# A hybrid SSD and MLP block on one core: the scheduler's order made with its other simulation

## The chip, the cores and the metric

The kernel runs on one core of a Trainium2 chip. The metric is the device time of one execution in microseconds, the median of several runs; a single profiled execution gives the trace and the profile.

## The reference

One decoder block over 512 tokens of width 1024: adaLN modulation from a vector c, RMSNorm, then a mixer of two branches (a Mamba-2 scan in 4 groups and 4 chunks of 128 tokens, and a causal pooling over four windows), gates, an output projection, a second norm, a squared-ReLU MLP of width 4096 and a last norm.

```python
mod = (silu(c) @ w_ada + b_ada); shift_m, scale_m, gate_m, shift_f, scale_f, gate_f = split(mod, 6)
h = rmsnorm(x, norm_mix_w) * (1 + scale_m) + shift_m
z, xbc, dt_raw, u_pool, gate_logits = split(h @ w_in)
xs, b, c = split(silu(causal_conv4(xbc)))
dt = softplus(dt_raw + dt_bias)
y = ssd_chunked_scan(xs * dt, -exp(a_log) * dt, b, c) + d_skip * xs      # 4 groups, 4 chunks
y_ssd = group_rmsnorm(y * silu(z)) @ w_branch_ssd
y_pool = causal_multiscale_pool(u_pool) @ w_branch_pool
x = x + gate_m * ((sigmoid(g_ssd) * y_ssd + sigmoid(g_pool) * y_pool) @ w_out)
h = rmsnorm(x, norm_mlp_w) * (1 + scale_f) + shift_f
x = x + gate_f * (relu(h @ w_up) ** 2 @ w_down)
return rmsnorm(x, norm_final_w)
```

## The kernel before

**Matrix products.** Channels lie on the partitions, tokens in the free dimension, so a product's output tile is 128 x 512 in one PSUM bank. Every product is three passes: both factors are split into a high part (a copy to fp32r) and a low part (the difference), and `mm3` (L155, L156, L157) adds high x high, high x low and low x high. A `unit` is one 128-column block of a weight: `load_unit` loads 1024 numbers per partition on SP (L140), makes the high part on ACT (L145, a cast) and the low part on DVE (L146), and PE then runs 24 matmuls, 8 slices by 3 passes. Activations are split in the same way by `split` (L125 on ACT, L126 on DVE).

**Stages.** A head (up to L332, about 60 us) makes h and the first seven products of w_in; its order is written by hand (`manual_schedule`). L353 to L377 turn the dt columns into dt (softplus by a series on DVE), into its running sums (PE L369 and transposes L373), and ACT (L374, L375) and SP (L376, L377) write these to two DRAM tables, `cs_d` and `ecs_d`. Then come the units of w_in with conv (ACT L395, DVE L397, ACT L412 for silu) and gate silu (L439), and between them the four groups of the scan. `ssd_group` loads for every chunk a broadcast of `cs_d` (SP L490), masks it (POOL L495), exponentiates it on ACT (L492, L494, and eight L499), multiplies by the scores on DVE (L500), transposes xs (PE L503), makes the chunk's state by one mm3, copies it (ACT L537 for the first chunk, into s_143 in group 0), and adds the output from the state of the chunk before (PE L529) and the one within the chunk (PE L549). L586 to L590 are the group's norm; `bs` (L457) multiplies by w_branch_ssd. Pooling, gates and w_out follow. The second norm is made in two halves of the tokens: PE L777 sums squares, ACT L779 and L780 make the factor, and for each of the eight slices of h DVE L806, ACT L807 and DVE L808 make the scaled, the high and the low part, h2[k]. The MLP starts with `up_first` and four plain units; the rest of w_up is multiplied by Strassen-like `Pair`s of seven products (`product`, L893; 12 matmuls of 256 columns), whose results go through ACT L1001 (relu), L1002 (square), a cast L834 and DVE L835 into `us`; `down_plain` (matmuls L155 to L157, then DVE L1082) multiplies `us` by w_down, once for each quarter of the hidden width. `last_down` ends with DVE L1100, the squares (ACT L1061, L1064, L1067, DVE L1065), the norm (PE L777, ACT L779, L780), four DVE multiplications L1107 for each half and the output DMAs L1108.

**What sets the order.** The program is written as calls in one order, each tile in a slot of the kernel's own lists (`Slots`, first in, first out). The tile framework then fixes an order for each engine and each queue: it simulates the program and takes, at each step, an instruction that is ready, by program order and by priority (`high_priority`, `issue_after`). On the chip each engine then runs its list strictly in turn and waits at an instruction until its inputs are there. The context has two simulations for this; the flag is read at L1190, and nothing else of the kernel is seen in the order. Slots and waits follow from the program, so that both orders use the same tiles.

```python
def prepare(c):                                          # in ssd_group
    sp.dma_start(m, cs_d[heads, cc].partition_broadcast(P))          # L490
    ...
    for i in range(HG):
        act.activation(m[:, i, :], m[:, i, :], AF.Exp, ...)          # L499
    dve.tensor_tensor(m, m, sc[:, cc]..., ALU.mult)                  # L500
...
for k in range(8):                                       # second norm, for each half
    dve.scalar_tensor_tensor(t, x1[k][:, t0:t1], amod..., R[:, t0:t1], ...)   # L806
    act.activation(hi, t, AF.Identity, bias=shift)                            # L807
    dve.scalar_tensor_tensor(lo, t, shift, hi.bitcast(F32), ...)              # L808
```

## Time and profile before

| what | value |
|---|---|
| runs | 966.47, 966.64, 968.96 us; median 966.64 |
| profiled execution | 965.36 us, span 963.6 us |
| granted clock of TensorE | 0.998 of full speed |
| instructions | 13261 |
| HBM read, written | 126.13 MB, 2.23 MB |

The page gives busy time by engine, the span in 40 slices, the chain of work that ended last, and groups of instructions by line; the trace behind it also answers with a timeline (start, duration from the first start to the last end of a row's instructions, engine, line, operation, output and inputs, count, and in brackets the idle time ahead of it with what ended it), with busy time by stretches, and with waits. PE is the TensorE matmul queue, PEld its weight loads, DVE VectorE, ACT ScalarE, POOL GpSimd, SP the queue that issues DMAs. Matmuls are pipelined: a row's duration is longer than the distance to the next start.

### The profile page before, as it was taken

Reading aid. Unit: us, or ns where it says so; the run is one execution under the profiler, and the core shown is the slowest. Engines: PE = TensorE matmul, PEld = TensorE weight load, DVE = VectorE, ACT = ScalarE, POOL = GpSimd, SP = SyncE. Lnnn points to the kernel's source line nnn. Section 1 sums busy time; section 2 is a strip of 40 time slices with the busy share of each in tenths; the row PEclk is TensorE's granted clock in tenths of the full one; section 3 lists DMA queues with packets and bytes.
Section 4 is the critical chain, followed back from the end, with each engine's and each line's share of the span. In section 5 each row is a group of like instructions: output and inputs, shape, how many; then the busy total and the mean of one; then the engine's idle time right before and its main releaser. Section 6 shows DMA issues by size and latency. Waiting matters only on the chain.

```text
span 963.6 us, 13261 instructions
## 1 busy us (share of the span) xinstructions
PE 950.4 (99%) x5135; PEld 804.5 (83%) x5135; DVE 657.7 (68%) x961; ACT 499.6 (52%) x811; POOL 89.6 (9%) x91
## 2 busy tenths in 40 slices
PE   8999999999999999999999999999999999999996
PEld 5877878888888888788888888998899889889986
DVE  7978868467766787987567574795557556664633
ACT  6479975657528542563312452684247127425732
POOL 0102321220212132300000000000000000000000
PEclk9999999999999999999999999999999999999999
DMA  9746433433253334446578463242144225214002
GB/s 369 298 132 182 130 99 121 131 110 110 76 161 113 98 101 132 158 153 210 181 241 281 127 208 120 94 143 75 45 145 130 66 76 165 89 33 154 23 1 88
DMA packets 61761, 129.22 MB, mean 134 GB/s; under 512 B 4673, under 2 KB 29505, under 8 KB 61698
## 3 DMA queue, kind: packets, MB, share of 16 engines
q1 hardware_dynamic: 61696, 128.38, 41.7%
q8 instruction: 40, 0.66, 0.3%
q14 instruction: 23, 0.19, 0.1%
q10 hardware_dynamic: 2, 0.00, 0.0%
HBM read 126.13 MB, written 2.23 MB: 133 GB/s over the span
## 4 chain that ended last, share of the span: by engine, by line
PE 84%; DVE 8%; ACT 3%; DMA 2%; issue 2%; POOL 0%; SPq 0%; DVEq 0%; ACTq 0%; POOLq 0%
PE ps L155 21%; PE ps L156 21%; PE ps L157 21%; PE ps L893 12%; PE ps L328 4%; DVE d L146 1%; PE ps L549 1%; DMA d<-cs_d 1%; DVE s L126 1%; PE ps L529 1%; DVE d L171 1%; DVE pad L631 1%; PE ps L503 1%; DMA d<-xp 1%; ACT d L145 1%
## 5 line engine op out<-in xcount | busy, mean ns | idle before, releaser
L155 PE MATMUL ps<-s,d 128*128 128x512 f32 (+1 forms) x1080 | 412.1, 382 | 1.1 <-ACT s L649 0.6
L156 PE MATMUL ps<-s,d 128*128 128x512 f32 (+1 forms) x1080 | 408.1, 378 | 0.2 <-DVE s L126 0.2
L157 PE MATMUL ps<-s,d 128*128 128x512 f32 (+1 forms) x1080 | 407.9, 378 | 0.0
L155 PEld LDWEIGHTS ps<-s,d 128*128 128x128 f32 x1080 | 202.7, 188 | 42.1 <-issue 2.2
L157 PEld LDWEIGHTS ps<-s,d 128*128 128x128 f32 x1080 | 202.7, 188 | 38.2 <-issue 0.2
L156 PEld LDWEIGHTS ps<-s,d 128*128 128x128 f32 x1080 | 202.8, 188 | 37.5 <-DVE s L126 0.7
L146 DVE TENSOR_TENSOR d<-d,d 128x1024 fp32r<-128x1024 f32 x88 | 112.4, 1278 | 61.6 <-ACT d L145 56.8
L145 ACT CAST d<-d 128x1024 fp32r<-128x1024 f32 x88 | 92.0, 1046 | 115.3 <-PE ps L156 74.7
L893 PE MATMUL ps<-s,d 128*128 128x256 f32 x864 | 103.8, 279 | 0.0
L893 PEld LDWEIGHTS ps<-s,d 128*128 128x128 f32 x864 | 102.9, 188 | 0.2
L834 ACT CAST d<-d 128x1024 fp32r<-128x1024 f32 x44 | 45.8, 1050 | 88.5 <-PE ps L156 62.8
L835 DVE TENSOR_TENSOR d<-d,d 128x1024 fp32r<-128x1024 f32 x44 | 53.5, 1223 | 27.4 <-ACT d L834 18.8
L834 ACT CAST d<-sz 128x1024 fp32r<-128x1024 f32 x32 | 33.7, 1052 | 68.9 <-PE ps L156 48.9
L1082 DVE SCALAR_TENSOR_TENSOR xs<-ps,mod,xs 128x512 f32<-128x512 f32 x29 | 21.8, 750 | 69.6 <-PE ps L157 69.6
L171 DVE CUSTOM_DVE_ANT_0 d<-d,d,par_t 128x1024 f32<-128x1024 f32 x32 | 41.8, 1307 | 27.3 <-DMA d<-adaT 27.2
L835 DVE TENSOR_TENSOR d<-sz,d 128x1024 fp32r<-128x1024 f32 x32 | 39.2, 1224 | 19.7 <-ACT d L834 16.4
L328 PE MATMUL ps<-s,d 128*128 128x512 f32 x168 | 40.1, 391 | 1.9 <-ACT s L316 1.9
L499 ACT ACTIVATE d<-d,ncs 128x128 f32<-128x128 f32 x128 | 39.9, 391 | 4.0 <-POOL d L495 4.0
L397 DVE SCALAR_TENSOR_TENSOR s<-ps,par_t,s 128x511 f32<-128x511 f32 (+2 forms) x54 | 39.7, 742 | 0.3
L328 PEld LDWEIGHTS ps<-s,d 128*128 128x128 f32 x168 | 31.4, 188 | 9.6 <-ACT s L316 2.4
L125 ACT CAST s<-s 128x512 fp32r<-128x512 f32 x32 | 19.7, 619 | 31.2 <-POOL s L511 18.7
L126 DVE TENSOR_TENSOR s<-s,s 128x512 fp32r<-128x512 f32 x32 | 25.7, 807 | 4.5 <-ACT s L125 4.5
(219 smaller groups left out, 1005.7 us busy)
## 6 DMA issues: line engine op xcount, KB each, us to landing
d<-adaT SPq DMA_DIRECT2D x32, 512.0 KB, 4.2
d<-wx SPq DMA_DIRECT2D x18, 512.0 KB, 3.6
d<-wdn SPq DMA_DIRECT2D x18, 512.0 KB, 3.9
d<-cs_d SPq DMA_DIRECT2D x16, 512.0 KB, 6.1
d<-wbs SPq DMA_DIRECT2D x16, 512.0 KB, 3.5
d<-wgate SPq DMA_DIRECT2D x16, 512.0 KB, 4.2
d<-wz SPq DMA_DIRECT2D x15, 512.0 KB, 3.5
sz<-wdn SPq DMA_DIRECT2D x14, 512.0 KB, 4.3
```

The source lines that it names most:

```text
L145: act.copy(hi[:, :w], r[:, a:a + w])
L146: (low or dve).tensor_tensor(lo[:, :w], r[:, a:a + w], hi[:, :w].bitcast(F32), ALU.subtract)
L155: pe.matmul(ps, whi, xhi[:, t0:t1], start=start, stop=False)
L156: pe.matmul(ps, whi, xlo[:, t0:t1], start=False, stop=False)
L157: pe.matmul(ps, wlo, xhi[:, t0:t1], start=False, stop=stop)
L171: dve.tensor_tensor_reduce(r, r, cbc, 1.0, col("b_ada", j), ALU.mult, ALU.add, mod[:, j:j + 1])
L328: pe.matmul(first[u], w[u][i // 2], h[k][i % 2], start=k == 0 and i == 0, stop=k == 7 and i == 2)
L397: dve.scalar_tensor_tensor(t[:, sh:], ps[:, :T - sh], w(3 - sh), t[:, sh:], ALU.mult, ALU.add)
L499: act.activation(m[:, i, :], m[:, i, :], AF.Exp, bias=ncs[:, c, g * HG + i:g * HG + i + 1])
L834: act.copy(dst[0], src)
L835: dve.tensor_tensor(dst[1], src, dst[0].bitcast(F32), ALU.subtract)
L893: pe.matmul(ps, x, y, start=start and m == 0 and i == 0, stop=m == 3 and i == 2, skip_group_check=True)
```

## The change

One argument at L1190: the context makes the order with its other simulation, the one that follows the queues in time. No instruction is added or removed by the program (the framework places 38 activation-table loads on ACT where it placed 36); what changes is the order on each engine and on SP's queue.

```diff
-    with tile.TileContext(nc) as tc:
+    with tile.TileContext(nc, schedule_with_timeline_sim=True) as tc:
         block_kernel(tc, out=out, **args)
```

The head keeps its order up to the first unit, and so do the last matmuls. In between some things move in every stage. In group 0 of the scan the whole chain L356 to L377 goes behind conv work, and PE's L369 from ahead of the unit of ps_118 to the end of that of ps_149; the DMAs L376, L377 and L490 go behind five weight loads; the L549 and L529 of the chunks go one or two units later, into the units of ps_192, ps_201 and ps_206; group 0's norm sum (L586) goes behind the first products of group 1. In groups 1 to 3 the L529 and L549 move up among the units of w_branch_ssd, and many sets are cut in pieces. In the second norm DVE takes eight L806 and then eight L808 where it took them by threes. In the Pair stages the products are taken in another order.

On ACT, in group 0, before: from the exponentials of the second chunk (d_130) to the copy L537 of the first chunk's state, and what stood behind it.

```order
L499 ACTIVATE d_130_742<-d_130_742,ncs 128x128
L145 CAST d_190_1103<-d_189_1101 128x1024
L499 ACTIVATE d_130_742<-d_130_742,ncs 128x128 x7
L125 CAST s_134_768<-s_133_766 128x512
L537 COPY s_143_813<-ps_142_809 128x512
L395 ACTIVATE s_150_864<-ps_149_839,par_t 128x512
L412 ACT_TABLE_LOAD
```

And now: the last twelve rows up to the same copy. Ahead of them stand, as before, the first chunk's exponentials (d_124) and the split L125 of s_128.

```order
L494 ACT_TABLE_LOAD
L494 ACTIVATE dec_80<-dec_80 128x8
L499 ACTIVATE d_130_742<-d_130_742,ncs 128x128 x8
L125 CAST s_134_768<-s_133_766 128x512
L499 ACTIVATE d_152_872<-d_152_872,ncs 128x128 x8
L145 CAST d_212_1247<-d_211_1245 128x1024
L125 CAST s_156_898<-s_155_896 128x512
L439 ACT_TABLE_LOAD
L439 ACTIVATE sz_178_1031<-ps_182_1038 128x512
L412 ACTIVATE xs_158_902<-s_163_934 128x512
L412 ACTIVATE xs_158_902<-s_174_1005 128x512
L537 COPY s_143_813<-ps_142_809 128x512
```

The copy L537, which stood right behind the second chunk's split (s_134), now has the third chunk's exponentials, two table loads, a weight cast and the silus L439 and L412 of later units ahead of it.

On PE, at the end of the first Pair stage, before: the last matmul of the last Pair's last product (ps_1082), and then the unit pair of down_plain (ps_1095 and ps_1096) from its first slices, us[0] (s_950, s_951), on.

```order
L893 MATMUL ps_1082_6377<-s_1007_5745,pad_1081_6323 128x256
L156 MATMUL ps_1095_6516<-s_951_5512,d_1086_6428 128x512
L157 MATMUL ps_1095_6516<-s_950_5511,d_1087_6429 128x512
L155 MATMUL ps_1096_6517<-s_950_5511,d_1089_6434 128x512
L156 MATMUL ps_1096_6517<-s_951_5512,d_1089_6434 128x512
L157 MATMUL ps_1096_6517<-s_950_5511,d_1090_6435 128x512
L155 MATMUL ps_1095_6516<-s_952_5513,d_1086_6428 128x512
```

And now: behind the same matmul stand the last two slices of that unit pair, us[6] (s_962, s_963) and us[7] (s_964, s_965); the rest of the unit pair has gone between the Pair's products.

```order
L893 MATMUL ps_1082_6377<-s_1007_5745,pad_1081_6323 128x256
L155 MATMUL ps_1095_6516<-s_962_5523,d_1086_6428 128x512
L155 MATMUL ps_1096_6517<-s_962_5523,d_1089_6434 128x512
L156 MATMUL ps_1095_6516<-s_963_5524,d_1086_6428 128x512
L157 MATMUL ps_1095_6516<-s_962_5523,d_1087_6429 128x512
L156 MATMUL ps_1096_6517<-s_963_5524,d_1089_6434 128x512
L157 MATMUL ps_1096_6517<-s_962_5523,d_1090_6435 128x512
L155 MATMUL ps_1095_6516<-s_964_5525,d_1086_6428 128x512
L155 MATMUL ps_1096_6517<-s_964_5525,d_1089_6434 128x512
L156 MATMUL ps_1095_6516<-s_965_5526,d_1086_6428 128x512
L157 MATMUL ps_1095_6516<-s_964_5525,d_1087_6429 128x512
```

us[7] is made from ps_1082, the product that ends in the first row of both. The second Pair stage ends in the same way; in the third, matmuls of `last_down` lie between.

On DVE, at the end of the kernel, before: from L1100 of the first half's last unit (ps_1286) to that of the second half's last unit (ps_1293).

```order
L1100 SCALAR_TENSOR_TENSOR xs_856_4818<-ps_1286_8261,mod,xs_856_4818 128x256
L1107 TENSOR_TENSOR xs_855_4817<-xs_855_4817,ps_1287_8289 128x2x256 x2
L1107 TENSOR_TENSOR xs_856_4818<-xs_856_4818,ps_1287_8289 128x2x256 x2
L1100 SCALAR_TENSOR_TENSOR xs_856_4818<-ps_1289_8303,mod,xs_856_4818 128x256
L1065 TENSOR_TENSOR s_1259_8024<-s_1259_8024,s_1290_8329 128x256
L1100 SCALAR_TENSOR_TENSOR xs_856_4818<-ps_1291_8333,mod,xs_856_4818 128x256
L1065 TENSOR_TENSOR s_1259_8024<-s_1259_8024,s_1292_8359 128x256
L1100 SCALAR_TENSOR_TENSOR xs_856_4818<-ps_1293_8363,mod,xs_856_4818 128x256
```

And now, from the same L1100 on:

```order
L1100 SCALAR_TENSOR_TENSOR xs_856_4818<-ps_1286_8261,mod,xs_856_4818 128x256
L1100 SCALAR_TENSOR_TENSOR xs_856_4818<-ps_1291_8333,mod,xs_856_4818 128x256
L1065 TENSOR_TENSOR s_1259_8024<-s_1259_8024,s_1292_8359 128x256
L1107 TENSOR_TENSOR xs_855_4817<-xs_855_4817,ps_1287_8289 128x2x256 x2
L1107 TENSOR_TENSOR xs_856_4818<-xs_856_4818,ps_1287_8289 128x2x256 x2
L1100 SCALAR_TENSOR_TENSOR xs_856_4818<-ps_1293_8363,mod,xs_856_4818 128x256
```

The four multiplications L1107 of the first half moved from ahead of the three last units' L1100 to just ahead of the last one; the unit of ps_1289 is taken earlier, right behind that of ps_1262.

## The prediction

> **What bounds the kernel now.** I read the page's busy shares first, then the busy time by stretch, then the waits of PE, and then, place by place, the timeline where the order of instructions changes. In the rows by stretch the columns are the stretch, its length, and for PE, PEld, DVE, ACT and POOL the busy us with the instructions; then the granted clock of TensorE.
>
> ```profile
> PE 950.4 (99%) x5135; PEld 804.5 (83%) x5135; DVE 657.7 (68%) x961; ACT 499.6 (52%) x811; POOL 89.6 (9%) x91
> ```
>
> ```profile
> 0.00:15.00 15.00, 11.85 (x32) 4.67 (x32) 9.70 (x21) 11.37 (x15) 0.99 (x7) 1.00 0.89 341
> 15.00:60.00 45.00, 44.79 (x196) 35.45 (x197) 39.87 (x59) 20.99 (x33) 5.58 (x8) 1.00 0.77 289
> 60.00:130.00 70.00, 69.40 (x372) 55.78 (x372) 60.29 (x104) 63.04 (x120) 18.65 (x18) 1.00 0.48 142
> 15.00:945.00 930.00, 927.67 (x5021) 789.88 (x5022) 640.30 (x927) 482.94 (x785) 88.57 (x84) 1.00 0.41 131
> 945.00:964.00 19.00, 10.93 (x86) 9.92 (x84) 7.66 (x14) 5.34 (x12) 0.00 (x0) 0.88 0.34 111
> ```
>
> PE is the bound from end to end. Of its idle time 3.15 us lie in the head (15.00 - 11.85), 8.07 in the tail (19.00 - 10.93) and only 2.33 in the 930 us between. The head is scheduled by hand and keeps its order, and the last PE instructions are the same. So an order can win about 2.3 us at most; it can lose without such a limit. From 60 to 130 us ACT is busy 63.04 of 70 us: there a step that is put behind others on ACT comes late.
>
> The profiled execution took 965.36 us (span 963.6), 1.28 under the median of the three runs, 966.64. I add differences to 965.36 and carry the sum to the median. About 0.3%, 2.9 us, is what a measurement of this kernel can tell from no change.
>
> **Group 0 of the scan.** Rows of PE, matmuls of 128x512 start 0.23 us apart, so a unit of 24 takes 5.44 us; the set of small products of L529 takes 0.81 us up to the next start, and the first matmul behind it 0.31 instead of 0.23.
>
> ```profile
> 97.32 0.39 PE L156 MATMUL ps<-s,d 128*128 128x512 f32 x1
> 97.55 0.39 PE L157 MATMUL ps<-s,d 128*128 128x512 f32 x1
> 97.77 1.05 PE L529 MATMUL ps<-s,s 128*128 128x128 f32 x8
> 98.58 0.48 PE L155 MATMUL ps<-s,s 128*128 128x512 f32 x1
> 98.89 0.40 PE L156 MATMUL ps<-s,s 128*128 128x512 f32 x1
> ```
>
> The first unit (ps_114) waits for the copy of one PSUM bank, which was the third of ACT's copies L385 and is now the fifth:
>
> ```profile
> 56.28 1.74 ACT L385 COPY s<-ps 128x512 f32<-128x512 f32 x3
> ```
>
> ```profile
> 58.07 0.50 PE L155 MATMUL ps<-s,d 128*128 128x512 f32 x1 [0.21 <-ACT s L385]
> ```
>
> Two copies of 0.5 more make that 58.95: **+0.9**.
>
> Then the chain of L353 to L377 (dt and its running sums) is moved behind conv work on DVE and ACT. PE's L369 comes behind 4 3/4 units and the small products (58.95 + 25.9 + 2.3 = 87.2), L373 half a unit further on (92.3), ACT's L374 behind a cast (93.2), and on SP the write L376 and the loads L490 now stand behind five weight loads, which have gone by then. Before, it ran like this:
>
> ```profile
> 71.06 0.57 ACT L374 ACTIVATE s<-ps 32x512 f32<-32x512 f32 x1
> ```
>
> ```profile
> 73.93 3.92 SPq L490 DMA_DIRECT2D d<-cs_d  x3
> ```
>
> ```profile
> 82.73 0.17 DVE L493 TENSOR_TENSOR dec<-d,ncs 128x8 f32<-128x8 f32 x1 [1.99 <-DMA d<-cs_d]
> ```
>
> From L374's end (71.63) to the first L490 it takes 2.3 us, to the second landing 11.1 (82.73). The page has 6.1 us as the middle time of such a load:
>
> ```profile
> d<-cs_d SPq DMA_DIRECT2D x16, 512.0 KB, 6.1
> ```
>
> In the new order ACT's L492 of the second load (d_130) stands ahead of L499 of the first (d_124). So L499 starts at 93.2 + 11.1 + 0.1 = 104.4 if the second load takes as long as before, at 102.4 with 6.1; I take 103.3. Behind it come, up to the copy L537 that gives s_143 to PE's L529 (ps_164), three sets of L499, three table loads, two casts L145, three L125, three L412 and one each of L395 and L439, where before L537 stood right behind the second set:
>
> ```profile
> 84.30 1.03 ACT L145 CAST d<-d 128x1024 fp32r<-128x1024 f32 x1
> 85.23 2.45 ACT L499 ACTIVATE d<-d,ncs 128x128 f32<-128x128 f32 x8
> 87.58 0.61 ACT L125 CAST s<-s 128x512 fp32r<-128x512 f32 x1
> ...
> 93.32 0.58 ACT L537 COPY s<-ps 128x512 f32<-128x512 f32 x1
> 93.79 0.78 ACT L395 ACTIVATE s<-ps,par_t 128x512 f32<-128x512 f32 x1
> 94.59 1.28 ACT L412 ACT_TABLE_LOAD   x1
> 95.88 0.64 ACT L412 ACTIVATE s<-s 128x512 f32<-128x512 f32 x1
> ```
>
> By start-to-start times that is 3x2.35 + 3x1.29 + 2x0.94 + 3x0.52 + 3x0.55 + 0.8 + 0.5 + 0.4 of small ones = 17.7, with L537's own 0.5 18.2 us: s_143 is there at 121.5. PE, for its part, needs s_129 for ps_142 at 108.8 and gets it 5.8 us after L499's start (the set, a cast and L125 on ACT 4.3, then L500 and L126 on DVE): 109.1, a wait of 0.3. From there to L529 of ps_164 lie 29 matmuls and the products of L549, 6.6 + 2.1 = 8.7 us: 117.8. It waits 121.5 - 117.8 = 3.7. Together **+4.0** (5.1 with 104.4; 3.2 with 102.4), less the **0.6** that PE was idle in 60:130 before. Behind L529 the queued units of group 0 wait as well: PE takes its instructions in order.
>
> [...]
>
> PE's order has 64 sets of small products between its units where it had 56. Each further change of form costs the 0.1 of the rows above: **+0.8**. Groups 1 to 3 also have products moved up among the wbs units, but there ACT's L537 stands right behind L395 and PE comes some us later than before, so I give them no wait.
>
> **The second norm (up_first).** DVE took three L806, then three L808; now it takes all eight L806 and an L760 before the first L808, whose result (the low half of h2[0]) is PE's fourth matmul of up_first.
>
> ```profile
> 606.19 0.70 PE L777 MATMUL ps<-sz,ones 128*128 128x256 f32 x2
> ```
>
> ```profile
> 606.98 0.47 ACT L779 ACTIVATE sz<-ps,eps_t 128x256 f32<-128x256 f32 x1 [1.31 <-PE ps L777]
> ```
>
> ```profile
> 607.94 1.28 DVE L806 SCALAR_TENSOR_TENSOR s<-xs,amod,sz 128x256 f32<-128x256 f32 x3 [1.81 <-ACT sz L780]
> 609.13 1.27 DVE L808 SCALAR_TENSOR_TENSOR s<-s,mod,s 128x256 fp32r<-128x256 f32 x3
> ```
>
> L779 to L806 takes 0.96 us; L779 starts 0.8 after L777. So the low half comes 1.75 + 9 x 0.4 + 0.45 = 5.8 us after L777, while PE now has 14 half matmuls of ps_923, the unit ps_924 and three matmuls in between: 41 at half of 0.23 and 0.1 for the change of form: 4.8. **+1.0**, less 0.3 that PE waited before L777 before.
>
> **The ends of the first two Pair stages.** The unit ps_1095/1096 of down_plain is begun early, between the products of the last Pair, so little is left behind the Pair's last product: PE wants s_964 after six matmuls, 1.36 us, where 38, 8.6 us, lay between. s_964 comes by L1001, L1002 and a cast:
>
> ```profile
> 743.52 0.60 ACT L1001 ACTIVATE pad<-ps 128x512 f32<-128x512 f32 x1
> 744.01 0.61 ACT L834 CAST s<-pad 128x512 fp32r<-128x512 f32 x1
> 744.52 0.64 ACT L1002 ACTIVATE pad<-pad 128x512 f32<-128x512 f32 x1
> ```
>
> 0.15 + 0.60 + 0.64 + 0.61 = 2.0 us after the product, so 0.65 too late (0.15 is my estimate of the step from PE to ACT; L779 above started 0.09 after L777's end). Its low half comes by DVE 0.7 later, with 0.45 of matmuls beside it: 0.25 more.
>
> ```profile
> 646.92 1.29 DVE L835 TENSOR_TENSOR s<-pad,s 128x512 fp32r<-128x512 f32 x2
> ```
>
> That is 0.9 in each of two stages: **+1.8**. In the third stage another unit lies between.
>
> **The tail.** DVE's four L1107 of the first half now stand ahead of L1100 of the second half's last unit, and ACT's L780 ahead of them behind an L1064 and L1067:
>
> ```profile
> 946.60 0.51 ACT L1067 ACTIVATE xs<-xs,par_t 128x256 f32<-128x256 f32 x1
> ...
> 947.83 0.37 ACT L780 ACTIVATE ps<-ps 128x256 f32<-128x256 f32 x1
> ```
>
> ```profile
> 948.23 2.48 DVE L1107 TENSOR_TENSOR xs<-xs,ps 128x512 f32<-128x512 f32 x4 [2.12 <-ACT ps L780]
> ```
>
> After the second L777 PE has 21 matmuls: L1100 could start 2.85 us after it. L779 (0.75) , L1067 (0.5), L780 (0.4), and four L1107 (2.4) put it at 4.55: **+1.7**, all of it on the path to the end.
>
> **Sum.** 0.9 + 4.0 - 0.6 + 0.8 + 1.0 - 0.3 + 1.8 + 1.7 = 9.3: 974.7 against the profiled execution, 975.9 at the level of the median. I say 976. With the bounds (waits of group 0 3.2 to 5.1, splits 0.3 to 1.6, the four later waits each up to 0.4 off) it lies between 973.5 and 979.
>
> **Rivals.** (1) Group 0's chain is ready in time, because loads and ACT are quicker than in the trace of before; the other places stay: 975.9 - 4.0 = 972, down to 971. For it: ACT is idle at times in that stretch (7 of 70 us). Against: 18 us of ACT rows stand in one queue. (2) The wait before L529 drops TensorE's clock. At the end PE's last matmul is over at 956.5 and the clock is
>
> ```profile
> 956.00:958.00 2.00, 0.52 (x2) 0.12 (x2) 0.56 (x1) 1.13 (x3) 0.00 (x0) 1.00 0.00 0
> 958.00:960.00 2.00, 0.00 (x0) 0.00 (x0) 1.92 (x4) 0.00 (x0) 0.00 (x0) 0.84 0.48 160
> 960.00:964.00 4.00, 0.00 (x0) 0.00 (x0) 0.00 (x0) 0.00 (x0) 0.00 (x0) 0.50 0.54 182
> ```
>
> 0.84 in 958:960 is full speed up to 959.4 and half from there, 2.9 us of idleness; a wait of 3.7 would reach it. If it took as long to come back as to fall, 2.9 us at half speed, 1.4 us are lost: 977.4, and up to 982 if other waits do it too. [...] (3) No change within 2.9 us: each of these waits is under a microsecond because the order was made by following the queues, and only tail and splits are left: 966.6 + 2.5 = 969. (4) Faster: the new order meets every wait of PE between 15 and 945 us and adds none. That is 2.33 us: 964.3, or 964.9 with the splits. It decides at L529 of ps_164: if ACT's copy L537 ends before PE gets there, and the tail's L1107 are done by L1100.
>
> **Numbers.** Forecast 0.55, rival 1 0.17, rival 2 0.14, rival 3 0.09, rival 4 0.05. Likeliest 976. The range 970.5 to 982 leaves out rivals 3 and 4 and the far end of 2. Faster by over 0.3% 0.03 (over half of rival 4), within 0.3% 0.11 (rival 3 and the rest of 4), slower 0.86.
>
> **What would show it.** Right: PE waits before L529 on ACT L537 near 120 us, for 3 to 4 us; before an L156 on DVE L808 near 620; before L155 on ACT L834 near 760 and 840; DVE's L1100 late behind L1107 at the end; the same busy time of PE. Wrong: PE idle under 3 us between 15 and 945, or waits in groups 1 to 3 or in the Pair stages before their ends.

## The result, and the profile after

The changed kernel took 998.35 us (median of 4 runs, 995.34 to 1000.24), the kernel before 966.56 beside it: a ratio of 1.0321, 95% interval 1.029 to 1.0352. It is 31.8 us slower where 9.3 were forecast and 982 was the end of the range. The profiled execution took 995.34 us (span 993.6), 30.0 more than that of before. Here are the page's busy shares, and then the stretches, with the columns of those of before:

```profile
PE 958.7 (96%) x5135; PEld 806.5 (81%) x5135; DVE 658.0 (66%) x961; ACT 502.4 (51%) x813; POOL 83.1 (8%) x91
```

```profile
60.00:130.00 70.00, 66.17 (x325) 53.23 (x325) 50.73 (x83) 50.19 (x91) 10.39 (x11) 0.98 0.45 126
130.00:220.00 90.00, 84.94 (x456) 68.47 (x454) 60.54 (x96) 60.26 (x116) 20.76 (x24) 0.98 0.38 109
220.00:640.00 420.00, 416.35 (x2058) 345.01 (x2058) 293.27 (x431) 193.38 (x295) 45.43 (x42) 1.00 0.47 145
640.00:740.00 100.00, 93.89 (x516) 81.76 (x516) 63.48 (x95) 48.21 (x75) 0.00 (x0) 0.97 0.32 98
740.00:970.00 230.00, 226.92 (x1458) 204.71 (x1457) 130.99 (x164) 111.07 (x176) 0.00 (x0) 1.00 0.28 85
```

PE was idle 2.33 us from 15 to 945 before; now it is idle 3.8 in the first of these stretches, 5.1 in the second, 6.1 in the fourth, and in those three the granted clock is below 1; in the two long ones it is idle 3.7 and 3.1. PE is also busy 8.3 us longer for the same 5135 matmuls. And ACT, which was busy 63.04 of the 70 us from 60 to 130, is now busy only 50.19: it stands still in the stretch in which the forecast had it full. The waits of PE, each with its total, its number and the longest:

```profile
PE ps L155 <- ACT pad L1001: 6.1, 1, 6.1
PE ps L586 <- ACT s L125: 5.5, 2, 4.9
PE ps L155 <- DVE s L397: 3.8, 1, 3.8
PE ps L155 <- ACT s L834: 2.0, 2, 1.0
...
PE ps L156 <- DVE s L126: 1.8, 2, 1.4
PE ps L777 <- ACT s L1061: 1.7, 1, 1.7
...
PE ps L155 <- ACT s L385: 1.2, 1, 1.2
PE ps L155 <- DVE s L459: 0.9, 1, 0.9
...
PE ps L156 <- DVE s L808: 0.2, 1, 0.2
```

The three long waits stand in none of the forecast's terms, and the one that it made the largest, L529 on ACT's L537, is not there. Read by the starts of neighbouring matmuls (what the distance is over the usual one, 0.227 us for 512 columns and 0.118 for 256), from 15 us on, the 30.0 us more are 22.9 in waits over 0.7 us (24.5 where there were 1.6), 4.8 in matmuls at half clock (none before) and 2.3 in small pieces.

**The first long wait**, on PE and then on DVE's timeline:

```profile
104.64 0.47 PE L155 MATMUL ps<-s,d 128*128 128x512 f32 x1 [3.83 <-DVE s L397]
104.94 0.40 PE L156 MATMUL ps<-s,d 128*128 128x512 f32 x1
105.18 0.43 PE L157 MATMUL ps<-s,d 128*128 128x512 f32 x1
105.41 0.63 PE L155 MATMUL ps<-s,d 128*128 128x512 f32 x1
```

```profile
97.26 0.75 DVE L397 SCALAR_TENSOR_TENSOR s<-ps,par_t,s 128x511 f32<-128x511 f32 x1 [0.21 <-ACT s L395]
100.39 0.17 DVE L493 TENSOR_TENSOR dec<-d,ncs 128x8 f32<-128x8 f32 x1 [2.38 <-DMA d<-cs_d]
100.47 1.40 DVE L397 SCALAR_TENSOR_TENSOR s<-ps,par_t,s 128x511 f32<-128x511 f32 x2
103.01 0.17 DVE L493 TENSOR_TENSOR dec<-d,ncs 128x8 f32<-128x8 f32 x1 [1.14 <-DMA d<-cs_d]
103.10 1.40 DVE L397 SCALAR_TENSOR_TENSOR s<-ps,par_t,s 128x510 f32<-128x510 f32 x2
```

The unit of ps_182 wants the bank of ps_149, which is free when the third L397 of that conv has read it. The first runs at 97.26. Ahead of the second stands an L493 whose load of cs_d lands at 100.4, and ahead of the third another, whose load lands at 103.0; each row x2 is an L397 of ps_162 and then this one of ps_149. So the third ends at 104.5, and PE goes on at 104.64. From 105.41 the matmuls are 0.63 us long instead of 0.39: half clock (granted 0.50 from 105.40 to 105.60).

**The second**, on ACT, ahead of the split (L125 of s_208) for which PE's L586 waits from 151.8 to 156.6:

```profile
142.02 2.44 ACT L499 ACTIVATE d<-d,ncs 128x128 f32<-128x128 f32 x8
144.36 1.04 ACT L145 CAST d<-d 128x1024 fp32r<-128x1024 f32 x1
145.41 1.28 ACT L439 ACT_TABLE_LOAD   x1
...
149.77 0.61 ACT L572 ACTIVATE s<-sz 128x512 f32<-128x512 f32 x1
...
150.58 0.61 ACT L572 ACTIVATE s<-sz 128x512 f32<-128x512 f32 x1
151.10 2.14 ACT L499 ACTIVATE d<-d,ncs 128x128 f32<-128x128 f32 x7
...
155.98 0.61 ACT L125 CAST s<-s 128x512 fp32r<-128x512 f32 x1
```

Group 0's last two squares (L572) and the split come behind group 1's first exponentials and behind the table loads between them.

**The third**, at the start of the MLP, on ACT and then on PE:

```profile
666.06 1.04 ACT L834 CAST d<-d 128x1024 fp32r<-128x1024 f32 x1 [1.36 <-PE ps L156]
667.01 0.59 ACT L1001 ACTIVATE pad<-ps 128x512 f32<-128x512 f32 x1
668.29 0.62 ACT L834 CAST pad<-pad 128x512 fp32r<-128x512 f32 x1 [0.69 <-DMA pad<-wup]
668.82 0.59 ACT L1001 ACTIVATE pad<-ps 128x512 f32<-128x512 f32 x1
...
671.71 0.60 ACT L1001 ACTIVATE pad<-ps 128x512 f32<-128x512 f32 x1 [0.24 <-DVE s L835]
```

```profile
672.36 0.79 PE L155 MATMUL ps<-s,d 128*128 128x512 f32 x1 [6.11 <-ACT pad L1001]
672.95 0.63 PE L156 MATMUL ps<-s,d 128*128 128x512 f32 x1
```

The L1001 at 671.71 frees the bank of ps_973. It comes after two older L1001 of up_first, which share its buffers, and these stand behind a weight cast that waits for PE to be done with its slot and a cast of a pad that waits for a load.

### The profile page after: what moved, and what is told of

The parts are those of the page before. It is cut to its first block, busy times and chain, and to the rows that moved or that the text cites. A ratio compares the mean times of both kernels' runs of the same rounds, so it can differ in the third digit from the quotient of the medians.

```text
span 993.6 us, 13282 instructions
## 1 busy us (share of the span) xinstructions
PE 958.7 (96%) x5135; PEld 806.5 (81%) x5135; DVE 658.0 (66%) x961; ACT 502.4 (51%) x813; POOL 83.1 (8%) x91
## 4 chain that ended last, share of the span: by engine, by line
PE 82%; ACT 6%; DMA 5%; DVE 4%; issue 1%; POOL 0%; SPq 0%; DVEq 0%; POOLq 0%; ACTq 0%
PE ps L155 21%; PE ps L156 21%; PE ps L157 21%; PE ps L893 12%; PE ps L328 4%; DMA d<-cs_d 3%; PE ps L549 2%; ACT d L499 1%; PE ps L529 1%; ACT d L145 1%; DMA d<-xp 1%; DMA pad<-wup 1%; PE ps L503 0%; DVE xs L1107 0%; ACT d L834 0%
## 5 line engine op out<-in xcount | busy, mean ns | idle before, releaser
L156 PE MATMUL ps<-s,d 128*128 128x512 f32 (+1 forms) x1080 | 410.0, 381 | 2.3 <-DVE s L126 1.8
L156 PEld LDWEIGHTS ps<-s,d 128*128 128x128 f32 x1080 | 203.8, 189 | 41.3 <-DVE s L126 2.9
L146 DVE TENSOR_TENSOR d<-d,d 128x1024 fp32r<-128x1024 f32 x88 | 109.4, 1243 | 51.6 <-ACT d L145 47.3
L893 PEld LDWEIGHTS ps<-s,d 128*128 128x128 f32 x864 | 102.7, 188 | 1.0
L893 PE MATMUL ps<-s,d 128*128 128x256 f32 x864 | 103.2, 279 | 0.0
L834 ACT CAST d<-d 128x1024 fp32r<-128x1024 f32 x44 | 45.8, 1049 | 86.2 <-PE ps L156 60.4
L835 DVE TENSOR_TENSOR d<-d,d 128x1024 fp32r<-128x1024 f32 x44 | 53.5, 1224 | 31.0 <-ACT d L834 23.2
L834 ACT CAST d<-sz 128x1024 fp32r<-128x1024 f32 x32 | 33.5, 1051 | 72.3 <-PE ps L156 42.3
L1082 DVE SCALAR_TENSOR_TENSOR xs<-ps,mod,xs 128x512 f32<-128x512 f32 x29 | 21.5, 750 | 60.5 <-PE ps L157 60.5
L499 ACT ACTIVATE d<-d,ncs 128x128 f32<-128x128 f32 x128 | 40.0, 389 | 12.4 <-POOL d L495 12.4
L328 PE MATMUL ps<-s,d 128*128 128x512 f32 x168 | 39.8, 391 | 1.9 <-ACT s L316 1.9
L397 DVE SCALAR_TENSOR_TENSOR s<-ps,par_t,s 128x511 f32<-128x511 f32 (+2 forms) x54 | 39.9, 742 | 0.6 <-ACT s L395 0.2
L328 PEld LDWEIGHTS ps<-s,d 128*128 128x128 f32 x168 | 31.5, 188 | 9.6 <-ACT s L316 2.4
L126 DVE TENSOR_TENSOR s<-s,s 128x512 fp32r<-128x512 f32 x32 | 25.6, 808 | 9.3 <-ACT s L125 9.0
L495 POOL TENSOR_SCALAR_AFFINE_SELECT d<-d 128x1024 f32<-128x1024 f32 x16 | 18.4, 1151 | 126.4 <-DVE dec L493 51.3
```

Source lines behind the costliest of these rows:

```text
L146: (low or dve).tensor_tensor(lo[:, :w], r[:, a:a + w], hi[:, :w].bitcast(F32), ALU.subtract)
L156: pe.matmul(ps, whi, xlo[:, t0:t1], start=False, stop=False)
L328: pe.matmul(first[u], w[u][i // 2], h[k][i % 2], start=k == 0 and i == 0, stop=k == 7 and i == 2)
L397: dve.scalar_tensor_tensor(t[:, sh:], ps[:, :T - sh], w(3 - sh), t[:, sh:], ALU.mult, ALU.add)
L499: act.activation(m[:, i, :], m[:, i, :], AF.Exp, bias=ncs[:, c, g * HG + i:g * HG + i + 1])
L834: act.copy(dst[0], src)
```

## The experiments

To change one thing at a time, the order itself was written out as a table of instruction numbers, engine by engine, and drawn as edges that fix the order of issue and make no wait (shortened; `ORDER` stands for the table):

```diff
+    for queue in ORDER:
+        for a, b in zip(queue, queue[1:]):
+            tc.add_manual_dep(traced[b], a, NoSync, reason="order")
```

Each kernel below differs from the changed one in the table alone, except the two with holds, which also have the old order. Rows outside the stretch that a table changes stand in the traces as in the changed kernel. The diffs of tables below are in words or by row names.

Two theories were set against each other. "Local": each long wait is one row that stands wrong in one queue; mended there, its time comes back. "Debt": group 0 of the scan is late as a whole, and a wait that is mended in one place comes back in the next.

**e1_front**

```diff
-every queue: changed order
+every queue: old order until the second cs_d load is in (83 us)
+             changed order from there
```

> The old order up to the second landing of the cs_d loads (some 83 us: the dt chain early), the changed order from there. Theory 'debt' (the late dt chain makes group 0 late as a whole, and both long waits of PE before 160 us, 3.8 us before an L155 on DVE L397 and 4.9 us before L586 on ACT L125, each with about 1.7 us at half clock, come of it): both go, and 1.0 of the first unit: 998.4 - 13.1 = 985.3. Theory 'local' (each long wait is one row that stands wrong in one queue, whenever it runs): only the first goes, with the first unit's: 998.4 - 6.5 = 991.9, and L586 still waits 4 to 5 us.

991.86 us (988.98 to 994.95), ratio 1.0264 (1.0238 to 1.0289): what "local" asks. (That it agrees to the tenth is luck: the four runs lie 6 us apart.) The late chain of dt makes the first long wait and the first unit's; L586 still waits 4.3 us.

**e2_conv**

```diff
 DVE
 L397 s_150<-ps_149
+L397 s_150<-ps_149
+L397 s_150<-ps_149
 L493 dec<-d_124
 L397 s_163<-ps_162
-L397 s_150<-ps_149
 L493 dec<-d_130
 L397 s_163<-ps_162
-L397 s_150<-ps_149
```

> The changed order, with two of DVE's L397 (conv of ps_149) ahead of the L493 that waits for cs_d. 'Local': the wait of 3.8 us and its half clock go: 998.4 - 5.5 = 992.9. 'Debt': PE is then 5.5 us earlier at s_129 and s_143, which come at 109.6 and 121.5 all the same, and waits about 1 us and 3.3 us there (before L529 of ps_164, as forecast): 998.4 - 1.2 = 997.2.

997.24 us (996.51 to 998.5), ratio 1.032 (1.0305 to 1.0336): "debt". (The tenth is luck here too: this trace has 3.41 us of half clock in the head, from 15 us on, that the changed kernel's has not.) The wait on L397 is gone from the trace, and the ones forecast in the prediction are there: 0.3 us at the split of s_129 and, on ACT and PE of this kernel,

```profile
121.82 0.57 ACT L537 COPY s<-ps 128x512 f32<-128x512 f32 x1
```

```profile
122.44 1.16 PE L529 MATMUL ps<-s,s 128*128 128x128 f32 x8 [2.70 <-ACT s L537]
```

So L537 does come about when it was worked out (121.5; it ends at 122.4 here and at 121.45 in the changed kernel), and PE had only been made later still by a wait that was overlooked. The row on DVE made that wait, but mending it alone is worth nothing beyond the scatter: the chain behind it is as late.

**e3_norm**

```diff
 PE
-L586 x2 (group 0)
 unit of ps_241
+L586 x2 (group 0)
```

> The changed order, with PE's two L586 of group 0 behind the unit ps_241 instead of ahead of it. 'Local': 4.9 us of wait and 1.7 at half clock go, and ys come when they did: 998.4 - 6.5 = 991.9. 'Debt': the units of wbs wait for ys instead, some us later: 998.4 - 2 = 996.4 or less gain.

995.27 us (992.75 to 999.06), ratio 1.0302 (1.0274 to 1.033), nearer to "debt": group 0's L586 no longer waits, and an L156 on DVE's L126 waits 3.0 that did not before. In this trace 2.3 us are gained where nothing was changed: the wait on L397 is 3.25 us and the clock stays up behind it, where the changed kernel's trace has 3.83 and 1.7 at half clock.

**e5_squares**

```diff
 ACT
 L499 d_244 x8
+L572 s_187
+L572 s_196
 L145 d_251
 L439
 L412 x2
+L125 s_208
 L494
-L572 s_187
 L499 d_267
-L572 s_196
 L499 d_267 x7
 L145 d_261
 L439
-L125 s_208
 DVE
+L126 s_209
 L146 d_262
-L126 s_209
```

> The changed order, with four rows of the first group's norm put earlier: on ACT the two squares L572 (s_187, s_196) behind the set of L499 instead of six and eight rows later, and L125 of s_208 ahead of the L494 and the set of L499 that it stood behind; on DVE L126 of s_209 ahead of one L146. 'Local': s_208 is there at about 150 us, before PE's L586 at 151.5, and ys come 6 us earlier with it: the wait of 5.0 and its half clock (1.4) go, 998.4 - 6.4 = 992.0, with no new wait at the units of wbs (which waited 3.2 us before L156 on DVE L126 when only L586 was moved). 'Debt': the ACT rows in between come late instead and PE waits for them (L500's results or ys): 996 or more.

995.63 us (994.32 to 996.02), ratio 1.0304 (1.0286 to 1.0322). Group 0's L586 no longer waits, and the time falls by 2.7 of the 6.4 us that "local" asks (here too the wait on L397 is shorter, 3.37 us, and at full clock). On PE and DVE:

```profile
169.22 0.80 PE L156 MATMUL ps<-s,s 128*128 128x512 f32 x1 [3.00 <-DVE s L126]
169.81 0.63 PE L157 MATMUL ps<-s,s 128*128 128x512 f32 x1
```

```profile
162.71 3.28 DVE L596 SCALAR_TENSOR_TENSOR sz<-sz,par_t,s 128x512 f32<-128x512 f32 x4
...
168.30 0.87 DVE L126 TENSOR_TENSOR s<-s,s 128x512 fp32r<-128x512 f32 x1
```

Group 0's four L596 stand on DVE ahead of the low half of group 1's first state input, so the same lateness is met some 13 us further on.

**e9_front165**

```diff
-every queue: changed order
+every queue: old order until group 0's ys are split (150 us)
+             changed order from there
```

> The old order until the last low half of group 0's ys (L126, some 150 us: the whole of group 0's scan and its norm), the changed order from there. 'Debt in group 0' (the two waits and what took their place when one was mended, all come of group 0's rows meeting group 1's on ACT and DVE): 13.5 us of waits and half clock before 170 us go, 998.4 - 13.5 = 984.9, and no wait over 2 us is left before 600 us. Rival: the changed order of group 1 makes such a wait by itself: 990 or more.

985.28 us (983.45 to 986.71), ratio 1.0194 (1.0178 to 1.0211): "debt in group 0". Behind the head no wait over 1.5 us is left before 600 us. With e1 this says that the dt chain's place is worth half of the 13.1 us, and the order of the rows from 83 to 150 us, in which group 0's end meets group 1's start, the other half. So neither theory holds alone: the first long wait goes when the dt chain is early, the second only with the rows around it. Which of those would have to move together was not tried.

**e4_mlp**

```diff
 ACT, DVE (second norm's end to the first plain units)
-changed order of L834, L1001, L1002, L835, L839 to L842, L870 to L876
+old order of the same rows
```

> The changed order, with ACT's and DVE's rows from the second norm's end to the first plain units (L834, L1001, L1002, L835, L839 to L842, L870 to L876) in their old order. Theory 'casts ahead': L1001 of ps_973 stands behind weight casts and a pad cast that wait for a slot and a load; with the old order it ends 11 us after up_first, PE is there after 9.3: a wait of 1.9 in place of 6.1 and full clock: 998.4 - 5.9 = 992.5. Rival 'loads': L868's pad and the casts' slots are late whatever the order: 998.4, within 1 us.

991.79 us (990.62 to 994.45), ratio 1.0271 (1.0249 to 1.0293): "casts ahead". PE waits there

```profile
669.23 0.50 PE L155 MATMUL ps<-s,d 128*128 128x512 f32 x1 [1.70 <-ACT pad L1001]
669.56 0.39 PE L156 MATMUL ps<-s,d 128*128 128x512 f32 x1
```

and goes on at full clock (0.39 us a matmul).

**e11_mlp**

```diff
-every queue: changed order
+every queue: old order until the first units of wout (570 us)
+             changed order from there
```

> The old order until the first units of wout (some 570 us), the changed order from there, so its MLP alone. By the waits of the changed kernel's trace: L1001 6.3 and 1.2 at half clock, the Pair ends 2.4, the tail 1.2: 966.6 + 11.1 = 977.7. Rival: the wait before L155 on ACT L1001 is handed down from the order before it, and goes with that: 970.

979.66 us (978.66 to 981.02), ratio 1.0138 (1.0123 to 1.0153). PE waits 6.6 us for L1001 here, 6.1 in the changed kernel: the MLP's part does not hang on what came before it.

**e6_ends**

```diff
 PE, ends of the first two Pair stages
-matmuls of down_plain's first two units between the Pair's products
+the same matmuls in the old order, behind them
 DVE
 L1107 x2
+L1100 ps_1293
 L1107 x2
-L1100 ps_1293
```

> The changed order, with PE's old order at the ends of the first two Pair stages (the matmuls of down_plain's first two units behind the Pair's last products), and DVE's last L1100 ahead of two of the four L1107. As forecast in mechanism: the two waits of 1.2 us before L155 on ACT L834 go, and the tail's wait before L777 falls from 2.0 to 0.85: 998.4 - 3.5 = 994.9. If these waits cover something else (weights or banks late): 998.4 within 1.

995.36 us (993.2 to 997.43), ratio 1.0304 (1.028 to 1.0327). The median looks like the expectation, but the runs lie 4.2 us apart, and the trace says otherwise for the stage ends: the two waits on L834 are gone, and in each stage a product waits instead for the sum L925,

```profile
768.04 2.15 PE L893 MATMUL ps<-s,d 128*128 128x256 f32 x16 [0.92 <-DVE ps L925]
```

which the early matmuls of down_plain had covered. On PE, the same 368 matmuls around the first stage's end take 58.06 us in the kernel before, 59.96 in the changed one and 59.19 here, and 505 around the second's 78.19, 80.12 and 79.33. So each end gains 0.8 of the 1.9 that it lost, and the tail 1.1: 2.7 in all.

**e7_all**: e1, e5, e4 and e6 together.

```diff
-changed order
+e1 up to 83 us, e5, e4, e6
```

> All repairs at once: the old order up to 83 us, the norm's four rows, the MLP's ACT and DVE rows in the old order, the ends. If the gains add up: 998.4 - 6.5 - 6.6 - 6.4 - 3.5 = 975.4, with no wait of PE over 2 us after 15 us and hardly any half clock; what is left over 966.6 is then small waits (some 5 us) and the splits. If waits only move on: 982 or more, with a new wait of several us in the trace.

980.29 us (978.86 to 981.29), ratio 1.0147 (1.0127 to 1.0166): 5 more than the sum. The trace has the waits of e5 and e6 that took the place of those mended: L156 on L126 3.0, with half clock behind it (0.63 us a matmul), and L893 on L925 1.9.

**e12_best**: the same without those two exchanges.

```diff
-changed order
+old order until group 0's ys are split (150 us), then the changed order
+e4
+DVE: L1100 ps_1293 ahead of two L1107
```

> The first 150 us and the MLP's ACT and DVE rows in the old order, DVE's last L1100 ahead of two L1107, the rest in the changed order, the Pair ends too. If the gains add up: 984.9 - 5.6 - 1.2 = 978; if a wait takes the place of one that is gone, more than 981.

976.69 us (975.59 to 977.2), ratio 1.0108 (1.0091 to 1.0125). The gains add up, and no matmul before the tail is at half clock in its trace (mean granted clock 0.998, as in the kernel before). Its longest waits of PE behind the head are

```profile
PE ps L155 <- ACT s L834: 2.0, 2, 1.0
...
PE ps L155 <- ACT pad L1001: 1.7, 1, 1.7
PE ps L156 <- DVE s L126: 1.4, 2, 1.1
```

It is the best that the experiments made of the changed order, and still slower than the kernel before. (Taking the stage ends of e6 in as well would gain another 1.6 by the traces; that was not run.) No version here beats the kernel before.

**e8_holds**: the price of a wait by itself, in the old order (shortened; `HOLDS` stands for the eight places).

```diff
+        probe = sb.tile([P, 128], F32, name="probe")
+        for y, x, n in HOLDS:
+            hold(tc, nc, probe, y, x, n)
+def hold(tc, nc, probe, y, x, n):
+    for k in range(n):
+        m = nc.gpsimd.memset(probe, 0.0).ins
+        if k == 0:
+            tc.add_manual_dep(m, x, Sync, reason="hold")
+    tc.add_manual_dep(traced[y], m.name, Sync, reason="hold")
```

> The old order, with eight holds of PE between 481 and 568 us, one ahead of every second unit: a chain of 4, 8, 11, 14, 17, 21, 27 and 35 idle POOL memsets of 128x128 that starts when PE is done and that PE waits for; about 0.5 + 0.2 each, 1.3 to 7.5 us, 30 in all, of which each wait costs its length. [...] Rival 'same again': the clock falls 2.9 us into a wait and takes as long to come back as it was down: losses that grow with the wait (0.5 to 2.3 each, 6 in all). Rival 'none': the waits alone, 996.6.

1017.5 us (1015.86 to 1019.51), ratio 1.054 (1.0515 to 1.0565). The holds came out longer than meant. PE's idle time in each, and the time from the start of the first matmul after it to that of the 25th (5.44 in an undisturbed unit):

| memsets | 4 | 8 | 11 | 14 | 17 | 21 | 27 | 35 |
|---|---|---|---|---|---|---|---|---|
| idle, us | 1.11 | 2.21 | 3.00 | 3.78 | 4.64 | 5.62 | 7.19 | 9.28 |
| next 24, us | 5.57 | 5.57 | 5.59 | 7.19 | 7.18 | 8.43 | 8.04 | 6.93 |

**e10_same**: the same with 14 memsets at all eight places.

> The old order with eight equal holds of PE, 14 memsets each (3.9 us as measured before), at the eight places. [...] Rival 'threshold': 3.9 us is beyond a limit between 3.2 and 3.9, so all eight fall: 1010. [...]

1015.05 us (1011.66 to 1015.62), ratio 1.0496 (1.0476 to 1.0516): what "threshold" asks, and dearer. After all eight the clock fell (24 matmuls in 7.19 to 8.10 us; mean granted clock 0.978), like this:

```profile
487.25 0.50 PE L155 MATMUL ps<-s,d 128*128 128x512 f32 x1 [3.73 <-POOL probe L1137]
...
487.93 0.63 PE L157 MATMUL ps<-s,d 128*128 128x512 f32 x1
```

The eight lost 2.1 us each on average (1.8 to 2.7) beside the wait. "Same again" falls with the table: 9.28 us of idleness cost 1.5. Why all eight fell was not shown.

## Why the prediction was wrong

The direction was right, and so was the account of PE as the bound, which an order can hardly help and can hurt without limit. The sum was 9.3 where 31.8 came. By the starts of the same matmuls in the two traces, the 30.0 us between them come about like this, with times of the old trace: 11.8 from 57 to 159 us (group 0), 6.7 from there to 440 (groups 1 to 3), 7.7 from 645 to 690 (the first plain units), 1.9 at each of two stage ends and 1.1 in the tail, less 1.1 in the head and from 440 to 645.

- **First unit**, +0.9 forecast: 1.2 on L385 against 0.2, so 1.0. Right.
- **Group 0**, +4.0 less 0.6: this step failed. It followed one chain, from the late cs_d loads through ACT's L499 and L537 to PE's L529, and put L537 at 121.5; e2 has its end at 122.4. But it asked only for the operands of PE's rows. The same loads also held DVE's L493, with the conv's L397 behind it, and L397 frees the PSUM bank that a unit needs. PE stands there from 100.8 to 104.6, some 17 us ahead of L529, and comes to L529 only at 123.13, when L537 has ended at 121.45: no wait. The second half of the group's price, L586 on the split behind ACT's L572, was not followed at all. Measured by e9 against the changed kernel, with the first unit's part: 998.35 - 985.28 = 13.1. (The forecast's 92.3 for L373 is not half a unit behind 87.2, which would be 89.9; the trace has 91.58, and nothing hangs on it.)
- **Clock**: the forecast had none and gave a rival 1.4 at L529. The rival was right that waits dropped the clock, and wrong on the place: after the three long waits, 3.83, 4.85 and 6.11 us idle, the next 24 matmuls took 7.16, 7.11 and 7.00 us, so about 1.6 to 1.7 were lost at each. They are counted in the 13.1 of group 0 and at L1001 below. Its 2.9 us of idleness, read off one fall in the tail, are no fixed time either, as the last section shows: the wait before L529 in e2, 2.70 us, dropped nothing, and at the three long waits the fall came 4.59, 4.81 and 2.35 us after PE had stopped.
- **Splits**, +0.8: about 1.0, counted as the excess distance at changes of form, of which the trace has 161 behind 58 us where it had 105 (waits and half clock left out). Right in size; the forecast counted sets of small products, and most of the new changes are between 512 and 256 columns.
- **up_first**, +0.7: L808 costs 0.2, and the L777 there nothing. Too much. What the forecast missed is 40 us on, and it is the second step that failed: "the other places stay" left the first plain units unchecked, where L1001 is late by 6.1 and 1.6 is lost at half clock. That it is the order of ACT's and DVE's rows there is shown by e4, in which 6.6 us come back.
- **Pair ends**, +1.8: 3.8. The mechanism is as forecast, at both places: 2.0 on L834 and 0.4 in each on its low half. What was missed is 0.4 in each on a bank that DVE's L1082 frees, and 0.2 in small pieces. Nor does it all come back when it is undone: in e6 a wait on L925 came in its place.
- **Tail**, +1.7: 1.7 before L777 where it was 0.6, so 1.1. The mechanism is right; the terms named, 0.75, 0.5, 0.4 and 2.4, make 4.05 and not 4.55, so the sum should have said 1.2.
- **Groups 1 to 3**, "no wait": 6.7. Three waits cost 0.8 to 1.7 by the distance of starts (L586, L459's bank, L126), 3.6 in all; the rest is smaller waits and changes of form. No experiment took these apart.

Rival 1 (the chain of group 0 in time) was wrong for the same reason as the forecast; e2's trace shows that the chain was not in time. Of the signs named ahead, the waits at L834 and the late L1100 came, and the one before L156 on L808 with 0.2; the one at L529 came only when the other was taken away. PE's busy time, which was to stay the same, grew by 8.3 us, most of it half clock and splits. The sign for "wrong" that came is waits in groups 1 to 3, and one on L1001 just ahead of the first Pair stage.

## What to carry to other kernels

When an order changes, look for rows that wait for a load and stand, in an in-order queue, ahead of rows that free a buffer: ask of every unit on the bounding engine not only when its operands come but who frees its bank, and what stands ahead of that row. Price such a wait with the stage behind it, since mending one of several late rows can give nothing back (e2) or move the wait on (e3, e5). And an idle stretch of the matmul engine has to be priced beyond its length: here the three long waits of the changed kernel (3.83 to 6.11 us), the five longest holds of e8 (3.78 to 9.28) and the eight of e10 (3.73 to 3.78) cost 1.5 to 3.0 us each behind them, and waits of 1.9 to 3.0 us were followed by half clock in some runs and by full clock in others.

## What the runs showed of the hardware

TensorE's granted clock was at half in four stretches of the changed kernel's trace, one at each of the three long waits and one from behind PE's last matmul on:

| PE waits for | L397 | L125, before L586 | L1001 | nothing more |
|---|---|---|---|---|
| PE idle, us | 100.81 to 104.64 | 151.79 to 156.64 | 666.25 to 672.36 | from 986.53 |
| clock at 0.50, us | 105.40 to 108.81 | 156.60 to 160.01 | 668.60 to 675.43 | from 989.45 |

So half clock lasted 3.41, 3.41 and 6.83 us at the waits, and at the end the fall came 2.92 us after PE had stopped. In the experiments, these are stretches around a hold of 3.00 us in e8, a hold of 3.73 us in e10, and the wait of 3.00 us in e5 (stretch, length, busy us of PE, PEld, DVE, ACT and POOL, granted clock, DMA):

```profile
506.87:510.28 3.41, 1.56 (x7) 0.94 (x6) 2.04 (x4) 1.04 (x1) 1.38 (x7) 1.00 0.90 304
510.29:513.69 3.40, 2.26 (x10) 1.87 (x11) 2.24 (x4) 0.00 (x0) 0.85 (x5) 1.00 0.69 254
```

```profile
484.28:487.69 3.41, 0.44 (x2) 0.40 (x3) 1.13 (x1) 0.59 (x2) 2.28 (x12) 1.00 0.64 256
487.70:491.10 3.40, 3.40 (x10) 2.61 (x9) 2.74 (x7) 0.00 (x0) 0.00 (x0) 0.50 0.60 186
```

```profile
165.07:168.48 3.41, 1.15 (x12) 0.67 (x8) 3.41 (x6) 1.48 (x3) 1.82 (x1) 1.00 0.00 0
168.49:171.89 3.40, 2.67 (x7) 2.08 (x8) 3.40 (x6) 2.72 (x4) 0.13 (x1) 0.50 0.81 260
171.90:175.30 3.40, 3.40 (x10) 2.63 (x9) 3.40 (x8) 0.00 (x0) 1.37 (x1) 0.50 0.54 137
```

Behind the hold of 3.00 us in e8 the clock stayed at 1.00; behind the wait of 3.00 us in e5 it was 0.50. The five holds of 3.78 us and more in e8 and all eight of e10 (3.73 to 3.78 us) had half clock behind them; the wait of 2.70 us before L529 in e2 and those of 3.25 to 3.37 us on L397 in e3, e4 and e5 had not. So the length of a wait alone does not tell the two kinds apart in these runs, and what does was not shown.

The loss is half of the half-clock time that PE then works through: 1.7, 1.7, 3.0, 2.7 and 1.4 us for the last five holds of e8, where the table's times are 1.75, 1.74, 2.99, 2.60 and 1.49 over 5.44; the granted clock in the 12 us around each was 0.86, 0.86, 0.73, 0.61 and 0.77. It does not grow with the wait (3.0 for 5.62 us of idleness, 1.4 for 9.28), since part of the half-clock time can lie within it, as the 3.76 us from 668.60 to 672.36 do in the changed kernel.

The changed kernel also scatters more, by 4.9 us over its 4 runs, the one before by 3.0 over 4. All 14 traces have a wait of 1.9 to 2.0 us before the head's L328; behind it the clock was at half for 3.41 us in e1, e2, e4, e7, e10 and e11, and at full speed in the others. Whether this is behind the scatter was not tried.
